# A two-layer decoder trunk on one core: the query transposes, two attention units, the value products and one bank choice are re-placed

## The chip, the core and the metric

The kernel runs on one core of a Trainium2 chip. The core has a matrix engine (TensorE, "PE" in the profile, with its weight loads shown apart as "PEld"), VectorE ("DVE"), ScalarE ("ACT"), GpSimd ("POOL") and SyncE ("SP"), which here only starts transfers. Each engine takes its instructions in the order of its own queue and waits where an operand or a buffer isn't ready. Matrix results go to an accumulator memory of eight banks; one bank holds 512 numbers of four bytes in each of 128 partitions. The metric is the device time of one execution in microseconds, lower is better.

## What is computed

Two layers over 256 tokens of width 2048, all in float32. In each layer one projection feeds a gated branch (A) and a windowed attention with 16 query heads on 4 key heads (B). Then follow an output projection and a SwiGLU block of width 5632.

```python
for l in range(DEPTH):
    h = rms_norm(x, norm1_g[l])
    z = h @ w_in[l]
    z_sgu = jax.nn.gelu(z[..., :2 * SGU_WIDTH], approximate=False)
    out_a = chunked_sgu(z_sgu, sgu_norm_g[l], sgu_w[l], sgu_b[l])
    out_b = swa_sink_attention(z[..., 2 * SGU_WIDTH:q_end], z[..., q_end:k_end],
                               z[..., k_end:], q_norm_g[l], k_norm_g[l], sinks[l],
                               rel_bias)
    mixed = jnp.concatenate([rms_norm(out_a, out_norm_a[l]),
                             rms_norm(out_b, out_norm_b[l])], axis=-1)
    x = x + mixed @ w_out[l]
    h2 = rms_norm(x, norm2_g[l])
    x = x + (jax.nn.silu(h2 @ w_gate[l]) * (h2 @ w_up[l])) @ w_down[l]
```

`chunked_sgu` normalizes its second half per head, multiplies it with a lower triangular 128x128 matrix per head (the gate product) and gates the first half with it. `swa_sink_attention` works in blocks of 128 queries: block 0 sees one block of keys, block 1 sees two; scores get a relative-position bias, the softmax has a sink term, and the value product follows.

## The kernel before, in words

**Products.** Every float32 weight tile of 256x512 is loaded (`raw`), rounded on ScalarE to a high part (`wh`, line 102), and VectorE takes the rest (`wl`, line 103). A product is three matmuls (lines 141 to 143). A unit (line 145) is one weight tile against two activations tiles and both token blocks: twelve matmuls of 512 columns. Each unit ends with `tick()`.

**Steps.** `later(delay, fn)` puts work into a list, and `tick` (line 124) runs what has come due, in order of time, then of entry. So the work between the large products is placed by unit counts. "Step k" below is the k-th unit after the first query block is done: 8 units for the second query block (steps 1 to 8), 8 each for the two blocks of the gate half (9 to 24), 8 each for the two blocks of the gated half (25 to 40), then the output projection. What is traced in this order is then put into queues by the language's scheduler, which may issue an instruction earlier where its operands and its buffer are free, and which assigns the slots of a tile's tag.

**The branch B.** `q_norm` (line 326) scales a query block, takes the inverse norms (a power on GpSimd, line 192), and transposes it in two pieces, five and six steps later (line 345); line 339 copies them out as `qT`. `attend(g, t)` (line 359) does group g of four heads on query block t: eight score matmuls into two half banks (lines 372 to 382), VectorE reads them with the bias (line 384), takes the maximum (389), ScalarE takes four exponentials (397), VectorE scales (406). `UNITS` (line 50) gives the step of each (g, t). After `LAG` = 5 steps `turn(b)` (line 408) transposes the probabilities of key block b into a bank, and ScalarE copies them out as `pts` (line 412). For each pair of groups `weigh(b)` (line 414) multiplies values and probabilities of both into `ov`, a bank of the `acc` tag, and `leave` (line 435) reads `ov` out with ScalarE and VectorE.

**The branch A.** `v_gate` (line 462) loads the triangular matrices (`wm`, lines 465 and 466), norms the block, and runs `spatial` (line 477) in two halves six and seven steps later: eight matmuls into `ps_g`, which VectorE reads in line 487. `u_gated` (line 502) transposes its result two and three steps later.

**The banks.** Five banks have the tag `acc`, two `dacc`, one `sm`. A projection block takes two `acc` banks, one for each token block. Everything small takes its bank from `small_ps` (line 136), which counts through `sm`, `dacc`, `acc`, `dacc`:

```python
pool, tag = ((pm, "sm"), (pd, "dacc"), (pa, "acc"), (pd, "dacc"))[next(turns) % 4]
```

So in one layer, steps 22 to 24 take in order: `s(2,1)` halves in `acc` and `dacc`, the first gate product in `sm`, the transposes of (2,0) in `dacc`, the second gate product in `acc` (step 23), the transposes of (3,0) in `dacc` (step 24), and then the next block's two `acc` banks. One layer counts 44 turns, so both layers meet the same banks.

**Buffers of attention.** The tag `spt` has four slots. Each unit takes one for its scores `s` (line 365); a unit with t = 1 takes a second one, `pt`, for its transposed probabilities (line 371).

**GpSimd's queue.** In order it holds the loads of the bias tiles (line 354; groups 2 and 3 come due with units (0,1) and (1,1)), of `wm`, and the powers of line 192.

Of the kernel before, what the change touches and what calls it, by code (L numbers as in the profile page):

```python
# [12 lines left out]
F32 = mybir.dt.float32  # L13
# [8 lines left out]
P = 128  # L22
D = 2048
SEQ = 256
NTOK = SEQ // P
L = 2
HD = 64
NH = 16
NKV = 4
GRP = NH // NKV  # L30
# [16 lines left out]
ACTS = 6  # L47
HOLD = 2
LAG = 5
UNITS = {(0, 0): 6, (1, 0): 8, (0, 1): 10, (1, 1): 13, (2, 0): 17, (3, 0): 19, (2, 1): 22, (3, 1): 26}  # L50
T3_DMA = ()
VEC = 1.14
VEC_P = 0.6
# [17 lines left out]
def trunk(ctx, tc, x, xt, w_in, w_out, w_gate, w_up, w_down, sgu_w, sgu_g, consts,  # L71
          rel_bias, onehot, radd, out):
    nc = tc.nc
# [8 lines left out]
    pa = ctx.enter_context(tc.tile_pool(name="pa", bufs=5, space=PSUM))  # L82
    pd = ctx.enter_context(tc.tile_pool(name="pd", bufs=2, space=PSUM))
    pm = ctx.enter_context(tc.tile_pool(name="pm", bufs=1, space=PSUM))
# [36 lines left out]
    def later(delay, fn):  # L121
        pending.append((clock[0] + delay, next(serial), fn))
# [10 lines left out]

    turns = itertools.count()

    def small_ps(shape, name):
        pool, tag = ((pm, "sm"), (pd, "dacc"), (pa, "acc"), (pd, "dacc"))[next(turns) % 4]
        return pool.tile(shape, F32, tag=tag, name=name)

    def mm3(acc, ah, al, wh, wl, first, last, **more):  # L140
# [142 lines left out]
    for lay in range(L):  # L283
# [11 lines left out]
        vhl = ap.tile([P, NTOK, NKV * HD], F32, tag="big", name="vhl", bufs=8)  # L295
# [30 lines left out]
        def q_norm(b, acc, lay=lay, layer=layer, qT=qT):  # L326
            qn = []
            for t in range(NTOK):
                z = zp.tile([P, NB], F32, tag="z", name="zq")
                nc.scalar.activation(z, acc[t], AF.Copy, scale=layer["rstd1"][t])  # L330
                qn.append(z)
            inv = head_inv(qn, 8)
            for t in range(NTOK):
                z3 = qn[t].rearrange("p (h d) -> p h d", d=HD)
                nc.vector.tensor_tensor(z3, z3, bc(inv[t], HD), ALU.mult)

            def to_T(c):
                ps = transpose_pair([qn[t][:, 2 * c * P : (2 * c + 2) * P] for t in range(NTOK)])
                nc.vector.tensor_scalar(
                    qT[b][:, 2 * c : 2 * c + 2, :], ps, cst[:, lay, C_QG : C_QG + 1], None,  # L340
                    ALU.mult,
                )

            for c in range(2):
                later(5 + c, lambda c=c: to_T(c))

        ov = {}
        sqs = zp.tile([P, 2 * NTOK, P], F32, tag="z", name="sqs")
# [8 lines left out]
        pts = {}  # L357

        def attend(g, t, kT=kT, qT=qT, vhl=vhl, ov=ov, bias=bias, layer=layer, pts=pts):
            nkb = t + 1  # L360
            nk = nkb * P
            k0 = SEQ - nk
            G = g // 2
            nsink = layer["nsink"]
            st = ap.tile([P, 2, GRP * P], F32, tag="spt", name="s", bufs=4)
            if t == 0:
                s = st[:, 0].rearrange("p (h k) -> p h k", k=nk)
                pts[g, t] = st[:, 1:2]
            else:
                s = st.rearrange("p b (h k) -> p (b h) k", k=nk)  # L370
                pts[g, t] = ap.tile([P, 2, GRP * P], F32, tag="spt", name="pt", bufs=4)
            halves = [small_ps([P, 2, nk], "ps_s") for r in range(2)]
            for i in range(2):
                for r in range(2):
                    h = g * GRP + 2 * i + r
                    nc.tensor.matmul(  # L376
                        halves[r][:, i, :],
                        qT[h // 8][HD * r : HD * r + HD, (h % 8) // 2, t * P : (t + 1) * P],
                        kT[HD * r : HD * r + HD, g, :nk],
                        start=True,  # L380
                        stop=True,
                    )
            for r in range(2):
                nc.vector.scalar_tensor_tensor(
                    s[:, r::2, :], halves[r], 1.0 / math.sqrt(HD), bias[g][:, r::2, k0:],
                    ALU.mult, ALU.add,
                )
            m = small([P, GRP], "m")
            nc.vector.tensor_reduce(m, s, AX.X, ALU.max)
            hs = slice(g * GRP, (g + 1) * GRP)  # L390
            nm = small([P, GRP], "nm")
            nc.vector.scalar_tensor_tensor(nm, m, -1.0, nsink[:, hs], ALU.mult, ALU.min)
            es = small([P, GRP], "es")
            nc.vector.tensor_tensor(es, nm, nsink[:, hs], ALU.subtract)
            den = small([P, GRP], "den")
            for i in range(GRP):
                nc.scalar.activation(
                    s[:, i, :], s[:, i, :], AF.Exp, bias=nm[:, i : i + 1],
                    accum_out=den[:, i : i + 1],
                )  # L400
            nc.scalar.activation(es, es, AF.Exp)

            rden = small([P, GRP], "rden")
            nc.vector.tensor_tensor(rden, den, es, ALU.add)
            nc.vector.reciprocal(rden, rden)
            nc.vector.tensor_tensor(s, s, bc(rden, nk), ALU.mult)

            def turn(b):
                pst = small_ps([P, GRP, P], "ps_p")
                for i in range(GRP):  # L410
                    nc.tensor.transpose(pst[:, i, :], s[:, i, b * P : (b + 1) * P], ident)  # L411
                nc.scalar.copy(pts[g, t][:, b], pst.rearrange("p h q -> p (h q)"))

            def weigh(b):
                if b == 0:
                    ov[G, t] = pa.tile([P, GRP * P], F32, tag="acc", name="ov")
                for k in range(2):
                    gk = 2 * G + k
                    nc.tensor.matmul(  # L419
                        ov[G, t][HD * k : HD * k + HD, :],  # L420
                        vhl[:, b, gk * HD : (gk + 1) * HD],
                        pts[gk, t][:, b],
                        start=b == 0,
                        stop=b == nkb - 1,
                        skip_group_check=True,
                    )
                if b == nkb - 1:
                    leave(G, t)

            for b in range(nkb):  # L430
                later(LAG + (2 if g % 2 else 1) * b, lambda b=b: turn(b))
                if g % 2:
                    later(LAG + 2 + 2 * b, lambda b=b: weigh(b))

        def leave(G, t, lay=lay, ov=ov, sqs=sqs, pairs_b=pairs_b):
            o = ov[G, t].rearrange("p (h q) -> p h q", q=P)
# [25 lines left out]
        def v_gate(b, acc, lay=lay, layer=layer, gate=gate):  # L462
            wm = ap.tile([P, 8, P], F32, tag="big", name="wm", bufs=8)
            with tc.issue_after(layer["anchor"].ins):
                nc.gpsimd.dma_start(wm, sgu_w[lay, :, 8 * b : 8 * b + 8, :])
            nc.gpsimd.affine_select(
                out=wm, in_=wm, pattern=[[0, 8], [1, P]], compare_op=ALU.is_ge, fill=0.0,
                base=0, channel_multiplier=-1,
            )
            gb = zp.tile([P, NB], F32, tag="z", name="gb")  # L470
            nc.gpsimd.dma_start(gb, sgu_g[lay, b * NB : (b + 1) * NB].partition_broadcast(P))

            v = ap.tile([P, NTOK, NB], F32, tag="big", name="v", bufs=8)
            vh = v.rearrange("p c (h d) -> p h c d", d=HD)
            gate[b] = v

            def spatial(half):
                hs = slice(4 * half, 4 * half + 4)
                ps = small_ps([P, 4, NTOK, HD], "ps_g")
                for h in range(4):  # L480
                    nc.tensor.matmul(
                        ps[:, h], wm[:, 4 * half + h, :], vh[:, 4 * half + h],
                        start=True, stop=True,
                    )
                sb = cst[:, lay, C_SB + 8 * b + 4 * half : C_SB + 8 * b + 4 * half + 4]
                for t in range(NTOK):
                    nc.vector.tensor_tensor(vh[:, hs, t], ps[:, :, t], bc(sb, HD), ALU.add)  # L487

            for t in range(NTOK):
                nc.scalar.activation(v[:, t], acc[t], AF.Gelu, scale=layer["rstd1"][t])  # L490
            inv = head_inv([v[:, t] for t in range(NTOK)], 8)
            for t in range(NTOK):
                v3 = v[:, t].rearrange("p (h d) -> p h d", d=HD)
                nc.vector.tensor_tensor(v3, v3, bc(inv[t], HD), ALU.mult)
                nc.vector.tensor_tensor(v[:, t], v[:, t], gb, ALU.mult)
            for half in range(2):
                later(6 + half, lambda half=half: spatial(half))
# [68 lines left out]
        acc = in_block(4)  # L566
# [339 lines left out]
```

## Time and profile before

| | us |
|---|---|
| time, median of 3 runs | 1936.86 |
| lowest and highest run | 1935.34 and 1938.22 |
| the profiled execution's own time | 1937.11 |
| its span in the profile | 1935.4 |

The span runs from the first to the last instruction; 1.7 us of the profiled execution lie around it. The profile gives busy time by engine, lists of who waited for whom, and a timeline of instructions; a row of the timeline has its start, its length, engine, line, operation, tiles and count, and in brackets the idle time just before it and what ended it. Rows of matmuls overlap, since they are pipelined, so the distance of two starts tells more than their length. The projection of layer 0 fills the span up to about 190 us, that of layer 1 about 985 to 1155 us, and the SwiGLU blocks take most of the rest.

### The profile page before, as it was taken

The page shows a single profiled execution, that of the slowest core. Times are in us where ns is not written, and L with a number is a line of the kernel's source. Part 1 is how long each engine was busy: PE and PEld are TensorE (multiplying, and loading weights), DVE is VectorE, ACT ScalarE, POOL GpSimd, SP SyncE. Part 2 cuts the span into 40 slices and gives each one's busy share as a digit, 9 for nine tenths or more (in the row PEclk, how much of TensorE's full clock was granted, in tenths as well). Part 3 has the DMA queues.
Part 4 walks back from the last instruction along what each step waited for, and adds up shares of the span by engine and source line. Part 5 has one row for each costly group of instructions (what it writes and reads, how often), then busy time and mean ns, then how long its engine had stood idle before and what let it go on. Part 6 is the DMA issues. An engine that isn't in the chain of part 4 may idle for free.

```text
span 1935.4 us, 24269 instructions
## 1 busy us (share of the span) xinstructions
PE 1923.8 (99%) x8734; PEld 1567.3 (81%) x8734; DVE 1699.1 (88%) x1896; ACT 1160.2 (60%) x1475; POOL 124.6 (6%) x127
## 2 busy tenths in 40 slices
PE   9999999999999999999999999999999999999999
PEld 7777888888888888888887788888888888888887
DVE  6787689999999999999767876899999999999995
ACT  7466566666565665656555665666665565665662
POOL 1210000000000000000012100000000000000000
PEclk9999999999999999999999999999999999999999
DMA  8744558668768777777655455576677678768773
GB/s 324 279 160 169 182 168 253 217 222 261 219 218 259 227 226 243 228 226 249 205 201 194 142 176 182 183 237 225 218 239 238 214 243 245 234 218 246 237 244 118
DMA packets 119704, 424.39 MB, mean 219 GB/s; under 512 B 13168, under 2 KB 15344, under 8 KB 119584
## 3 DMA queue, kind: packets, MB, share of 16 engines
q1 hardware_dynamic: 106928, 377.57, 54.0%
q0 software_dynamic: 12512, 45.19, 12.4%
q8 instruction: 68, 1.11, 0.2%
q14 instruction: 52, 0.43, 0.1%
q10 hardware_dynamic: 144, 0.08, 0.0%
HBM read 420.66 MB, written 4.23 MB: 220 GB/s over the span
## 4 chain that ended last, share of the span: by engine, by line
PE 96%; DVE 2%; ACT 1%; DMA 0%; issue 0%; SPq 0%; ACTq 0%; DVEq 0%
PE m L142 11%; PE m L143 11%; PE m L141 11%; PE acc L141 10%; PE dacc L141 10%; PE dacc L142 10%; PE acc L143 10%; PE acc L142 10%; PE dacc L143 10%; PE ps_f L214 1%; DVE wl L103 1%; PE ps_s L376 1%; PE ov L419 1%; PE ps_p L411 1%; PE ps_n L214 1%; ACT wh L102 0%
## 5 line engine op out<-in xcount | busy, mean ns | idle before, releaser
L102 ACT CAST wh<-raw 128x1024 fp32r<-128x1024 f32 (+1 forms) x778 | 799.0, 1049 | 583.5 <-DVE raw L674 198.8
L103 DVE TENSOR_TENSOR wl<-raw,wh 128x1024 fp32r<-128x1024 f32 (+1 forms) x778 | 926.4, 1219 | 131.1 <-ACT wh L102 125.3
L142 PE MATMUL dacc<-wl,aT 128*128 128x512 f32 x576 | 225.5, 391 | 0.0
L141 PE MATMUL dacc<-wh,aT 128*128 128x512 f32 x576 | 225.2, 392 | 0.0
L142 PE MATMUL m<-wl,ext 128*128 128x512 f32 x576 | 225.0, 391 | 0.0
L143 PE MATMUL dacc<-wh,aT 128*128 128x512 f32 x576 | 224.7, 390 | 0.0
L141 PE MATMUL m<-wh,ext 128*128 128x512 f32 x576 | 224.7, 392 | 0.0
L143 PE MATMUL m<-wh,ext 128*128 128x512 f32 x576 | 224.5, 390 | 0.0
L103 DVE TENSOR_TENSOR wl<-t,wh 128x1024 fp32r<-128x1024 f32 x144 | 175.6, 1222 | 25.0 <-ACT wh L102 21.3
L102 ACT CAST wh<-t 128x1024 fp32r<-128x1024 f32 x144 | 151.2, 1051 | 57.8 <-PE dacc L143 39.6
L141 PE MATMUL acc<-wh,hT 128*128 128x512 f32 x448 | 179.7, 402 | 2.2 <-DVE v L487 2.0
L142 PE MATMUL acc<-wl,hT 128*128 128x512 f32 x448 | 175.3, 391 | 1.2 <-DVE wl L103 1.2
L143 PE MATMUL acc<-wh,hT 128*128 128x512 f32 x448 | 175.3, 391 | 0.0
L141 PE MATMUL m<-wh,hT 128*128 128x512 f32 x432 | 168.6, 390 | 0.1
L143 PE MATMUL m<-wh,hT 128*128 128x512 f32 x432 | 168.2, 389 | 0.0
L142 PE MATMUL m<-wl,hT 128*128 128x512 f32 x432 | 168.2, 389 | 0.0
L141 PE MATMUL acc<-wh,aT 128*128 128x512 f32 x384 | 152.1, 396 | 0.0
L143 PE MATMUL acc<-wh,aT 128*128 128x512 f32 x384 | 150.1, 391 | 0.0
L142 PE MATMUL acc<-wl,aT 128*128 128x512 f32 x384 | 149.8, 390 | 0.0
L686 POOL DMA_DIRECT2D t<-in_w_gate_dram x72 | 61.5, 854 | 1325.9 <-DVE wl L103 828.0
L141 PEld LDWEIGHTS dacc<-wh,aT 128*128 128x128 f32 x576 | 108.2, 188 | 24.1 <-DVE xres L766 1.4
L142 PEld LDWEIGHTS dacc<-wl,aT 128*128 128x128 f32 x576 | 108.2, 188 | 24.0 <-DVE wl L103 2.2
(150 smaller groups left out, 2811.0 us busy)
## 6 DMA issues: line engine op xcount, KB each, us to landing
raw<-in_w_gate_dram SPq DMA_DIRECT2D x176, 512.0 KB, 5.4
raw<-in_w_up_dram SPq DMA_DIRECT2D x176, 512.0 KB, 4.5
raw<-in_w_down_dram SPq DMA_DIRECT2D x176, 512.0 KB, 4.9
raw<-in_w_in_dram SPq DMA_DIRECT2D x108, 512.0 KB, 4.2
t<-in_w_gate_dram POOLq DMA_DIRECT2D x72, 512.0 KB, 6.5
raw<-in_w_out_dram SPq DMA_DIRECT2D x64, 512.0 KB, 3.2
bias<-rdram POOLq DMA_DIRECT2D x8, 512.0 KB, 6.5
raw<-in_w_in_dram SPq DMA_DIRECT2D x8, 256.0 KB, 5.1
```

The source lines that it names most:

```text
L102: nc.scalar.copy(wh[:, j : j + step, :], src)
L103: nc.vector.tensor_tensor(wl[:, j : j + step, :], src, f(wh[:, j : j + step, :]), ALU.subtract)
L141: nc.tensor.matmul(acc, ah, wh, start=first, stop=False, **more)
L142: nc.tensor.matmul(acc, ah, wl, start=False, stop=False, **more)
L143: nc.tensor.matmul(acc, al, wh, start=False, stop=last, **more)
L214: nc.tensor.transpose(ps[:, j, t * P : (t + 1) * P], blocks[t][:, j * P : (j + 1) * P], ident)
L376: nc.tensor.matmul(halves[r][:, i, :], qT[h // 8][HD * r : HD * r + HD, (h % 8) // 2, t * P : (t + 1) * P], kT[HD * r : HD * r + HD, g, :n ...
L411: nc.tensor.transpose(pst[:, i, :], s[:, i, b * P : (b + 1) * P], ident)
L419: nc.tensor.matmul(ov[G, t][HD * k : HD * k + HD, :], vhl[:, b, gk * HD : (gk + 1) * HD], pts[gk, t][:, b], start=b == 0, stop=b == nkb - ...
L686: nc.gpsimd.dma_start(t2, w_gate[lay, b, i, 1], accum_op=ALU.add)
```

## The change

Four edits. The query transposes come four and five steps after `q_norm` instead of five and six. Unit (0,0) moves from step 6 to 5, unit (1,1) from 13 to 14; the load of group 3's bias comes due with the latter. The transposes of the second key block follow one step after the first for all groups (it was two for odd ones), and the value products of both key blocks run together, in one step, one step after the last transposes. The gate product passes `False` to `small_ps`, which then passes over a turn that falls on `acc`.

```diff
-UNITS = {(0, 0): 6, (1, 0): 8, (0, 1): 10, (1, 1): 13, (2, 0): 17, (3, 0): 19, (2, 1): 22, (3, 1): 26}
+UNITS = {(0, 0): 5, (1, 0): 8, (0, 1): 10, (1, 1): 14, (2, 0): 17, (3, 0): 19, (2, 1): 22, (3, 1): 26}
...
-    def small_ps(shape, name):
-        pool, tag = ((pm, "sm"), (pd, "dacc"), (pa, "acc"), (pd, "dacc"))[next(turns) % 4]
+    def small_ps(shape, name, spare=True):
+        at = next(turns) % 4
+        if at == 2 and not spare:
+            at = next(turns) % 4
+        pool, tag = ((pm, "sm"), (pd, "dacc"), (pa, "acc"), (pd, "dacc"))[at]
         return pool.tile(shape, F32, tag=tag, name=name)
...
             for c in range(2):
-                later(5 + c, lambda c=c: to_T(c))
+                later(4 + c, lambda c=c: to_T(c))
...
-            def weigh(b):
-                if b == 0:
-                    ov[G, t] = pa.tile([P, GRP * P], F32, tag="acc", name="ov")
-                for k in range(2):
-                    gk = 2 * G + k
-                    nc.tensor.matmul(
-                        ov[G, t][HD * k : HD * k + HD, :],
-                        vhl[:, b, gk * HD : (gk + 1) * HD],
-                        pts[gk, t][:, b],
-                        start=b == 0,
-                        stop=b == nkb - 1,
-                        skip_group_check=True,
-                    )
-                if b == nkb - 1:
-                    leave(G, t)
+            def weigh():
+                ov[G, t] = pa.tile([P, GRP * P], F32, tag="acc", name="ov")
+                for b in range(nkb):
+                    for k in range(2):
+                        gk = 2 * G + k
+                        nc.tensor.matmul(
+                            ov[G, t][HD * k : HD * k + HD, :],
+                            vhl[:, b, gk * HD : (gk + 1) * HD],
+                            pts[gk, t][:, b],
+                            start=b == 0,
+                            stop=b == nkb - 1,
+                            skip_group_check=True,
+                        )
+                leave(G, t)
 
             for b in range(nkb):
-                later(LAG + (2 if g % 2 else 1) * b, lambda b=b: turn(b))
-                if g % 2:
-                    later(LAG + 2 + 2 * b, lambda b=b: weigh(b))
+                later(LAG + b, lambda b=b: turn(b))
+            if g % 2:
+                later(LAG + 1 + nkb, weigh)
...
-                ps = small_ps([P, 4, NTOK, HD], "ps_g")
+                ps = small_ps([P, 4, NTOK, HD], "ps_g", False)
```

## The prediction, made before the changed kernel was built

> **What bounds the kernel now.** I read the page first: busy time by engine and the chain that ended last.
>
> ```profile
> PE 1923.8 (99%) x8734; PEld 1567.3 (81%) x8734; DVE 1699.1 (88%) x1896; ACT 1160.2 (60%) x1475; POOL 124.6 (6%) x127
> ...
> PE 96%; DVE 2%; ACT 1%; DMA 0%; issue 0%; SPq 0%; ACTq 0%; DVEq 0%
> ```
>
> TensorE works or streams for 1923.8 of 1935.4 us. The change removes no matmul, so it can only move the 11.6 us in which TensorE stood. Busy TensorE could hide slow spots, so I looked at the distance of starts in a plain stretch, and then at who TensorE waited for and at stretches around those waits.
>
> ```profile
> 1098.16 0.39 PE L141 MATMUL acc<-wh,hT 128*128 128x512 f32 x1
> 1098.39 0.39 PE L142 MATMUL acc<-wl,hT 128*128 128x512 f32 x1
> ...
> PE acc L141 <- DVE v L487: 2.0, 1, 2.0
> PE ps_t L214 <- DVE s L384: 1.7, 1, 1.7
> PE heat L172 <- DVE mhalf L174: 1.5, 1, 1.5
> PE acc L142 <- DVE wl L103: 1.2, 2, 0.6
> ...
> PEld ps_t L214 <- ACT s L412: 0.5, 1, 0.5
> ...
> 98.00:100.60 2.60, 0.86 (x5) 0.40 (x4) 2.53 (x5) 2.01 (x3) 0.88 (x2) 1.00 0.92 314
> 100.60:140.00 39.40, 39.40 (x204) 29.73 (x205) 34.23 (x64) 24.71 (x63) 5.62 (x4) 1.00 0.47 159
> 1100.50:1103.00 2.50, 0.47 (x3) 0.16 (x2) 2.22 (x9) 2.02 (x8) 0.00 (x0) 1.00 0.13 51
> 1900.00:1935.40 35.40, 30.89 (x137) 25.25 (x135) 15.56 (x18) 7.37 (x7) 0.00 (x0) 0.98 0.23 80
> ```
>
> A product takes 0.23 us from start to start; a unit of twelve is 2.7 us. (Columns of the last four rows: length, then busy us of PE, PEld, DVE, ACT, POOL, then granted clock.) Of the 11.6 us, 4.5 are the end of the kernel and 1.5 its beginning, out of reach. Within reach are two waits: 1.7 us, a query transpose that waits for VectorE to read scores (layer 0, step 14), and 2.0 us, the second bank of a new projection block, which waits for the gate product's read (layer 1, step 24). In both stretches VectorE is nearly full (2.53 of 2.60, 2.22 of 2.50): the bank is free late because VectorE takes its queue in order and comes late. So the ceiling is 1.74 + 2.03 = 3.8 us, or some 4.1 with the short wait for line 412 at step 14 of layer 1 (0.5 on the weight loads, about 0.3 of it in the products).
>
> **Layer 0: transposes earlier, (1,1) later.**
>
> ```profile
> 87.83 0.60 PE L411 MATMUL ps_p<-ident,s 128*128 128x128 f32 x4
> 95.40 0.60 PE L214 MATMUL ps_t<-ident,zq 128*128 128x128 f32 x4
> 100.48 0.66 PE L214 MATMUL ps_t<-ident,zq 128*128 128x128 f32 x4 [1.74 <-DVE s L384]
> ...
> 90.48 1.29 DVE L335 TENSOR_TENSOR zq<-zq,ir 128x512 f32<-128x512 f32 x2 [2.19 <-POOL ir L192]
> ...
> 99.75 1.28 DVE L384 SCALAR_TENSOR_TENSOR s<-ps_s,bias 128x512 f32<-128x512 f32 x2
> 100.94 0.74 DVE L339 TENSOR_SCALAR qT<-ps_t,cst 128x512 f32<-128x512 f32 x1
> ```
>
> The second transpose wants one of two `dacc` banks; one still holds the scores of (1,1), read from 99.75 on. With the transposes at steps 12 and 13 and (1,1) at 14 they no longer meet: -1.74. What is late next is the transposes' operand. Step 11 starts at 87.83, its four transposes take 0.36, so step 12 ends near 87.83 + 0.36 + 2.72 = 90.9, and VectorE finishes the scaled queries at 90.48 + 1.29 = 91.8, having waited 2.19 for GpSimd's power. That is a new wait of 0.9 at most; it is 0 if (0,0), a step earlier, takes its exponentials out of ScalarE's way before the query block is read. I take 0.5. The scores of (1,1) at step 14 (near 97.0) now want a `dacc` bank that step 12's transposes left; line 339 came 5.5 us after its transposes (95.40 to 100.94), so from 91.8 it would end at 98.1: 0 to 0.5 after the half that wants it, and I take 0, since it then stands ahead of (1,1)'s work. Layer 0: **-1.2**, from -1.7 to -0.3.
>
> **Layer 1: the bank counts shift.** Passing over `acc` uses up a turn, twice in layer 0 (second gate product of each block), so layer 1 starts two turns off and its small tiles sit in other banks than those of layer 0. Counted through the steps: the scores of (2,0) at step 17 start in `acc`; (3,0) at 19, and (2,1) at 22, start in the single `sm`; the first gate product is in `dacc`, the transposes of (2,0), same step, in `sm`, the second gate product in `dacc`; the transposes of (3,0) at 24 are in `acc`.
>
> ```profile
> 1078.78 0.71 PE L376 MATMUL ps_s<-kT,qT 64*128 64x128 f32 x8
> 1083.39 0.66 PE L411 MATMUL ps_p<-ident,s 128*128 128x128 f32 x4
> 1092.70 0.60 PE L411 MATMUL ps_p<-ident,s 128*128 128x128 f32 x4
> 1099.53 0.60 PE L411 MATMUL ps_p<-ident,s 128*128 128x128 f32 x4
> 1102.87 0.47 PE L141 MATMUL acc<-wh,hT 128*128 128x512 f32 x1 [2.03 <-DVE v L487]
> ...
> 1090.53 0.75 DVE L384 SCALAR_TENSOR_TENSOR s<-ps_s,bias 128x256 f32<-128x256 f32 x2
> 1097.30 1.28 DVE L384 SCALAR_TENSOR_TENSOR s<-ps_s,bias 128x512 f32<-128x512 f32 x2
> 1105.10 0.35 DVE L450 SCALAR_TENSOR_TENSOR aT<-ov,cst,aT 128x128 fp32r<-128x128 f32 x1
> 1106.75 0.58 ACT L412 COPY s<-ps_p 128x512 f32<-128x512 f32 x1
> ```
>
> Step 24: the wait for the gate product goes, -2.03. But the five `acc` banks then hold the old block (2), `ov` of (0,1) and the transposes of (3,0); the new block finds one bank, and its second one must come from `ov` (read until 1105.10 + 0.35) or from those transposes (copied until 1107.3), where it is due near 1100.6. If VectorE and ScalarE are as late as now, that is up to 4.8 in place of 2.03; the lower end is 0. For the choice I look at what makes VectorE late: TensorE gave the scores of (3,0) at 1078.78, and VectorE read them at 1090.53. Their `spt` slot explains it: in use are the scores of (1,1) (until their transposes at 1083.39), `pt` of (0,1) and of (1,1), and the scores of (2,0). After the change `pt` of (1,1) is first written at step 19, not 18, so (3,0) can take the fourth slot at once and its chain may start up to 4 us (1083.4 - 1079.4) sooner. So the read of `ov` should come sooner too; I take 1.0 for steps 22 to 24, nearer the low end.
>
> ```profile
> 1071.98 0.71 PE L376 MATMUL ps_s<-kT,qT 64*128 64x128 f32 x8
> ...
> 1072.55 0.69 ACT L490 ACTIVATE v<-acc,ir 128x512 f32<-128x512 f32 x1
> ```
>
> Step 17: two old banks, `ov` of (0,0) and two new ones fill `acc`, and the scores of (2,0) wait until ScalarE has read an old one: 1072.55 + 0.69 - 1071.98 = 1.3 at most, 0 if ScalarE comes sooner because (1,1)'s exponentials have moved; I take 0.6. Layer 1: -2.03 + 1.0 + 0.6 = **-0.4**, from -2.3 to +4.1.
>
> **What costs nothing.** The joined value products are the same matmuls; one place less per layer where small work breaks the stream is worth at most one product's distance, so 0 to -0.5 in all, taken as 0. The moved load and GpSimd's queue:
>
> ```profile
> 1023.99 1.54 POOL L354 DMA_DIRECT2D bias<-rdram  x2
> ...
> 1062.60 0.53 POOL L465 DMA_DIRECT2D wm<-in_sgu_w_dram  x1 [2.51 <-DVE s L384]
> 1066.57 1.54 POOL L466 TENSOR_SCALAR_AFFINE_SELECT wm<-wm 128x1024 f32<-128x1024 f32 x1 [3.43 <-DMA wm<-in_sgu_w_dram]
> ...
> 1076.84 2.92 POOL L192 TENSOR_TENSOR ir<-ms,mhalf 128x16 f32<-128x16 f32 x1 [8.73 <-DVE ms L190]
> ```
>
> Groups 2 and 3's bias leave at 1023.99, some 30 us before (1,1): they go when a slot is free, not at their step. The second `wm` load does wait for (1,1)'s read; a step (about 3.1 us) later its mask ends at 1071.2 instead of 1068.1, still ahead of the power at 1076.84, behind which nothing moves. Without that cover the power and VectorE behind it would be late by the rest.
>
> **Sum.** -1.2 - 0.4 = -1.6 on the profiled execution's 1937.11: **1935.5 us**. The median of the runs is 0.25 lower, well inside their spread, so I leave it there.
>
> **Rivals.** *All of it goes.* If no new wait opens, -4.1: 1933.0. For it: every new wait above has a lower end of 0, and layer 0's banks at step 24 are free. Against: VectorE's lateness isn't removed, only put before other banks.
>
> *The bank is filled again.* The gate product leaves the fifth bank and the transposes of (3,0) take it at step 24 of layer 1; the wait there stays at about 2, step 17 adds its 1.3, layer 0 gives -1.2: 1937.2. For it: the count of turns. Against: the earlier start of (3,0).
>
> *Slower: one bank twice in one step.* In layer 1, step 22 puts the scores of (2,1) and the transposes of (2,0) into the single `sm` bank. TensorE reached those transposes at 1092.70; VectorE read the first half of the scores until 1097.30 + 0.6 = 1097.9. A queue that is placed as now stands 5.2 us there, after which step 24 finds its bank free. With step 17's 1.3 and layer 0's -1.2: 1937.1 + 5.2 + 1.3 - 2.0 - 1.2 = 1940.4, and 1941.6 if layer 0 gives nothing. It is slower than before from a wait of 3.2 less step 17's part. For it: both rows; against: the scheduler may place the next unit's products ahead of those transposes. [...]
>
> **Numbers.** The forecast (some gain, partly given back) has 0.38 with a range of its own of 1933.5 to 1938; all of it goes 0.22; the bank is filled again 0.15; slower 0.25. 0.2% is 3.9 us, about what a measurement of this kernel can tell from no change. Below 1933.0 lie most of the second case's better half and a little of the forecast: 0.18. Above 1940.7 lie half of the slower case, 0.13, and 0.04 for what this reading doesn't foresee: 0.17. The rest, 0.65, is within. The range for 8 in 10 is 1932.4 to 1941.2.
>
> **What would show it.** Right: no wait of a query transpose for line 384 in layer 0, step 14; a short wait near step 12 with GpSimd's power behind it; no wait of `acc` for line 487; in layer 1 small waits at steps 17 and 22 to 24 on lines 490, 450 or 412; line 384 of (3,0) sooner after its scores. Wrong: a TensorE wait above 3 us at step 22 of layer 1 (slower case), no wait in either layer (the second case), or a change of time outside the two projections, which nothing here foresees.

## The result and the profile after

| | us |
|---|---|
| after, median of 12 runs | 1932.34 (1931.2 to 1933.7) |
| before, median of 12 runs on the same chip | 1936.35 (1934.72 to 1939.8) |
| ratio, 95% interval | 0.9979, 0.9972 to 0.9986 |
| the profiled execution after, its span | 1932.53, 1930.8 |

The change gains 4.0 us, 0.21%. The forecast was 1935.5, with 1932.4 as its low end: the sign was right, the size was not, and the time lies 0.06 us below the range. It is the first rival ("all of it goes", 1933.0) that came.

The page of the changed kernel: span, and busy time by engine.

```profile
span 1930.8 us, 24275 instructions
PE 1922.1 (100%) x8734; PEld 1568.0 (81%) x8734; DVE 1698.7 (88%) x1896; ACT 1162.8 (60%) x1475; POOL 122.8 (6%) x127
```

What TensorE waited for in it (total, times, longest):

```profile
PE heat L175 <- DVE mhalf L177: 1.5, 1, 1.5
PE acc L145 <- DVE wl L103: 1.1, 2, 0.6
PE acc L144 <- ACT pt L415: 0.4, 1, 0.4
PE dacc L144 <- ACT wh L102: 0.4, 1, 0.4
PE ps_p L414 <- DVE s L387: 0.4, 1, 0.4
```

Both long waits are gone. Three short ones, 0.4 each, came new: for `pt` and for `s` in the two projections, and for `wh` outside them, at 309.7 us. (Lines after the edit of `small_ps` count three higher: 387 reads scores, 415 copies `pt`.) The two stretches that the prediction showed, in its columns:

```profile
98.00:100.60 2.60, 2.60 (x15) 1.87 (x15) 2.60 (x3) 1.04 (x1) 0.00 (x0) 1.00 0.61 195
1100.50:1103.00 2.50, 2.50 (x12) 2.07 (x12) 2.46 (x4) 2.19 (x3) 0.00 (x0) 1.00 0.55 205
```

TensorE no longer stops in either, while VectorE is as full as it was (2.60 of 2.60, 2.46 of 2.50). It has not become faster; it comes sooner to what TensorE needs. Layer 1's timeline, steps 19 to 22, shows where:

```profile
1076.54 0.72 PE L379 MATMUL ps_s<-kT,qT 64*128 64x128 f32 x8
1086.46 1.14 PE L379 MATMUL ps_s<-kT,qT 64*128 64x256 f32 x8
1087.53 1.94 PE L422 MATMUL ov<-pt,vhl 128*64 128x512 f32 x8
1089.40 1.16 PE L483 MATMUL ps_g<-v,wm 128*128 128x128 f32 x8
1090.91 0.66 PE L414 MATMUL ps_p<-ident,s 128*128 128x128 f32 x4 [0.36 <-DVE s L387]
...
1080.13 0.42 DVE L387 SCALAR_TENSOR_TENSOR s<-ps_s,bias 128x256 f32<-128x256 f32 x1
1090.17 1.28 DVE L387 SCALAR_TENSOR_TENSOR s<-ps_s,bias 128x512 f32<-128x512 f32 x2
```

The scores of (3,0) are read 3.59 us after TensorE starts them (1076.54 to 1080.13; before 1078.78 to 1090.53, 11.75), those of (2,1) 3.71 us after (before 1089.50 to 1097.30, 7.80). Below, "the lag" of a unit is this distance, in layer 1. From the first transposes of k to the sum of squares at the end of the branch, layer 0 takes 132.70 us (before 134.54) and layer 1 145.18 (before 148.26). That is -1.8 and -3.1; the rest of the program changes by less than 0.4. Against a second profile of the kernel before (before_again, below) it is +0.1 and -4.7: how the gain divides between the layers depends on the execution.

### The profile page after: what moved, and what is told of

Same layout as the page of the kernel before. It is cut to its first block, busy times and chain, and to the rows that moved or that the text cites. A ratio compares the mean times of both kernels' runs of the same rounds, so it can differ in the third digit from the quotient of the medians.

```text
span 1930.8 us, 24275 instructions
## 1 busy us (share of the span) xinstructions
PE 1922.1 (100%) x8734; PEld 1568.0 (81%) x8734; DVE 1698.7 (88%) x1896; ACT 1162.8 (60%) x1475; POOL 122.8 (6%) x127
## 4 chain that ended last, share of the span: by engine, by line
PE 94%; DVE 3%; ACT 1%; issue 1%; DMA 1%; POOL 0%; SPq 0%; ACTq 0%; DVEq 0%; POOLq 0%
PE m L145 11%; PE m L146 11%; PE m L144 11%; PE dacc L144 10%; PE dacc L145 10%; PE dacc L146 10%; PE acc L144 9%; PE acc L146 9%; PE acc L145 9%; DVE wl L103 1%; PE ps_f L217 1%; PE ps_n L217 1%; PE ps_s L379 0%; PE ps_p L414 0%; PE ov L422 0%
```

## The experiments

Each run was compared with the kernel before on the same chip; its medians there were 1936.38, 1937.16 and 1937.63 in the three groups, so ratios compare better than times. The layers' columns are the lengths just defined, from the profiled execution.

| run | median us (runs) | ratio, 95% interval | layer 0 | layer 1 | lag (3,0) | lag (2,1) |
|---|---|---|---|---|---|---|
| moves_only | 1945.84 (5) | 1.0049, 1.0035 to 1.0063 | 140.64 | 150.83 | 3.59 | 6.46 |
| join_only | 1933.73 (11) | 0.9985, 0.9976 to 0.9994 | 132.10 | 146.70 | 7.54 | 6.79 |
| bank_only | 1941.07 (11) | 1.0024, 1.0015 to 1.0033 | 132.59 | 153.97 | 10.44 | 6.54 |
| all_but_bank | 1931.41 (8) | 0.9974, 0.9964 to 0.9984 | 132.60 | 144.62 | 3.59 | 3.71 |
| split_early | 1940.63 (11) | 1.0017, 1.0008 to 1.0025 | 138.04 | 148.02 | 3.74 | 2.37 |
| join_late | 1938.59 (11) | 1.0010, 1.0001 to 1.0019 | 137.15 | 148.82 | 3.75 | 7.72 |
| split_late | 1940.13 (11) | 1.0014, 1.0005 to 1.0023 | 137.51 | 149.19 | 3.77 | 7.45 |
| join_first | 1932.99 (8) | 0.9976, 0.9966 to 0.9986 | 133.46 | 145.64 | 7.05 | 6.76 |
| join_second | 1934.00 (8) | 0.9976, 0.9966 to 0.9986 | 133.59 | 145.95 | 4.19 | 4.31 |
| join_bank | 1941.34 (12) | 1.0018, 1.0010 to 1.0026 | 134.58 | 153.91 | 6.25 | 6.76 |
| before_again | 1936.64 (1) | none | 132.57 | 149.84 | 11.75 | 7.80 |
| after_again | 1932.22 (1) | none | 132.76 | 145.19 | 3.60 | 3.71 |

Theory A: VectorE came late because (3,0) had to wait for a slot of `spt`, and the moves end that. Theory B: the wait in layer 1 is only the gate product's place in `acc`, and the bank edit ends it.

**moves_only**: the query transposes and the two units, nothing else.

```diff
-UNITS = {(0, 0): 6, (1, 0): 8, (0, 1): 10, (1, 1): 13, (2, 0): 17, (3, 0): 19, (2, 1): 22, (3, 1): 26}
+UNITS = {(0, 0): 5, (1, 0): 8, (0, 1): 10, (1, 1): 14, (2, 0): 17, (3, 0): 19, (2, 1): 22, (3, 1): 26}
...
-                later(5 + c, lambda c=c: to_T(c))
+                later(4 + c, lambda c=c: to_T(c))
```

> Only the query transposes and the units (0,0) and (1,1) are moved; value products split and gate product in acc as before. Both theories: the wait of 1.7 us in layer 0 (query transposes for the read of scores) goes, about -1.8 us in layer 0. Theory A (VectorE's lateness, caused by the missing fourth spt slot, makes the wait of layer 1): (3,0) finds its slot at step 19 and is read under 5 us after its scores, but the last value products come at step 23 and hold slots and ov longer, so the wait at step 24 of layer 1 is between 0 and 3 us. Theory B (the wait of layer 1 is only the gate product's place in acc): it stays at 2.0 us. Time 1933 to 1936 by A, 1934.5 by B.

It is 9.5 us slower than before: both theories miss the time. No wait at step 24 came, which B had at 2.0 and A between 0 and 3. The timeline around step 21 of layer 0 (TensorE, and ScalarE's copy):

```profile
123.23 1.07 PE L419 MATMUL ov<-pt,vhl 128*64 128x512 f32 x2
124.24 0.66 PE L411 MATMUL ps_p<-ident,s 128*128 128x128 f32 x4
...
127.53 1.07 PE L419 MATMUL ov<-pt,vhl 128*64 128x512 f32 x2 [1.71 <-ACT pt L412]
...
126.90 1.06 ACT L412 COPY pt<-ps_p 128x512 f32<-128x512 f32 x2
```

Now (3,0) takes the free slot (lag 3.59, as A said), and `pt` of (1,1) must wait for the slot that (1,1)'s own scores hold until their second transposes at 124.24. With the split order, these come at step 21 together with the value product of the first key block, half of which stands and waits. The two copies then leave ScalarE in one go, at 126.90, behind the exponentials of (3,0) in its queue. The scores of (2,1), a step behind, find the slots held until step 23: VectorE stands idle for 3.34 us and reads them only when the last value product is done.

```profile
135.91 1.08 PE L419 MATMUL ov<-pt,vhl 128*64 128x512 f32 x4
...
137.03 1.29 DVE L384 SCALAR_TENSOR_TENSOR s<-ps_s,bias 128x512 f32<-128x512 f32 x2 [3.34 <-PE ov L419]
```

From that comes a second wait, 2.16 in each layer, of the second block's gate product (step 30). And here two matmuls of a value product take 1.01 us (123.23 to 124.24), since the pairs of the two groups are torn apart. In the kernel before, four, both groups together, take as long (1090.69 to 1091.70):

```profile
1090.69 1.08 PE L419 MATMUL ov<-pt,vhl 128*64 128x512 f32 x4
1091.70 1.16 PE L481 MATMUL ps_g<-v,wm 128*128 128x128 f32 x8
```

**join_only**: transposes at `LAG + b`, value products in one step (the change's hunk of `weigh`).

> Only the value products are joined; (1,1) then has its second transposes at step 19 instead of 20. Both theories: the 1.7 us wait of layer 0 stays. Theory A: the slot for the scores of (3,0) comes free a step sooner, they are read some 3 us sooner than before, and the wait at step 24 of layer 1 falls from 2.0 to under 0.7 us. Theory B: it stays at 2.0 us, since the gate product is still in acc. Time near 1934 by A with fewer places where small work breaks the stream, near 1936 by B.

0.9985. No wait at step 24 is left, as A had it. The second transposes of (1,1) come one step sooner, so does the last value product (step 21, not 22), and the slots with them: the lag of (3,0) falls from 11.75 to 7.54. The wait of layer 0 is gone too, which neither theory had; see before_again.

**bank_only**: the change's hunk of `small_ps` and its call.

> Only the gate product passes over acc. Both theories: the 1.7 us wait of layer 0 stays. Theory A: VectorE is as late as before, so in layer 1 a wait of 1.5 us or more comes at steps 22 to 24 in another bank (the transposes of (2,0) in sm, or the new block's acc). Theory B: the 2.0 us go and nothing comes in their place. Time 1936 to 1939 by A, 1934.4 by B.

The wait came as theory A said; the time lies 2 us above its range. What TensorE waited for:

```profile
PE ps_p L414 <- DVE s L387: 4.0, 1, 4.0
PE heat L175 <- DVE mhalf L177: 1.5, 1, 1.5
PE ps_s L379 <- ACT v L493: 1.4, 1, 1.4
```

This is the prediction's slower rival, with its two waits at steps 22 (priced 5.2, came 4.04) and 17 (priced 1.3, came 1.44). Windows behind the long one, in the prediction's columns, the granted clock third from the end:

```profile
1093.00:1097.00 4.00, 0.78 (x5) 0.78 (x5) 4.00 (x6) 1.78 (x4) 0.00 (x0) 0.74 0.39 126
1097.00:1101.00 4.00, 4.00 (x12) 3.13 (x11) 3.21 (x8) 2.46 (x9) 0.00 (x0) 0.50 0.44 137
```

Twelve matmuls in 4.00 us instead of 2.7, at a granted clock of 0.50: the wait costs some 2 us more than its length, an estimate from half of these 4.00 us.

**all_but_bank**: the changed kernel with the gate product back in `acc` (`small_ps([P, 4, NTOK, HD], "ps_g")`).

> The changed kernel with the gate product in acc again. Theory A: VectorE is in time, the gate product's read comes right after its matmuls, and step 24 of layer 1 waits under 0.5 us; time as the changed kernel, 1932 to 1933. Theory B: the wait of about 2 us at step 24 of layer 1 is back; time near 1934.4.

0.9974 (1931.41, 0.6 below A's range), no wait at step 24: B falls. Against join_only in the same group the moves are worth 2.3 us here; against moves_only the joined products are worth 14.4. Its interval overlaps that of the whole change, so the bank edit is worth nothing that was measured; without it the wait of 0.36 at step 22 is absent.

What was left: is it the time at which slots come free (theory C), or the fewer stops of joined products (theory D)? Three kernels, all with the moves and the earlier transposes and without the bank edit, shift or split the value products of the units with t = 1: joined at step 22 is all_but_bank.

**split_early**: `weigh(b)` as in the kernel before, its blocks at steps 21 and 22.

```diff
-            if g % 2:
-                later(LAG + 1 + nkb, weigh)
+                if g % 2:
+                    later(LAG + 2 + b, lambda b=b: weigh(b))
```

> The moves with the transposes of (1,1) at steps 19 and 20 as in the changed kernel, but its value products split again: the first block at step 21, the second at 22; gate product in acc as before. Theory C (release): what counts is when the four spt slots come free, and whether a value product stands ahead of the transpose that frees its own slot. Here the slots come free at step 22 as in the kernel without the bank edit (1931.41), so (3,0) is read within 4.5 us of its delivery, (2,1) within 5, and no gate product waits for VectorE; but ScalarE copies pt of (1,1) at 125.9, behind the exponentials of (3,0), and the first value product, due near 123.3, has to wait some 1 to 2.7 us for it in each layer: 1933.5 to 1937.5. Theory D (fewer stops): the joined products are worth their stops, and without them the time is that of the moves alone, 1944 to 1947.

The lags came as C said, and so did the wait of the first value product (2.02 and 1.60), with none at the gate product. But the time is 3 us above C's range. One part is the torn pair, 1.0 in each layer, the other the clock behind the 2.02, granted at 0.52:

```profile
129.00:132.00 3.00, 3.00 (x9) 2.37 (x8) 1.46 (x2) 0.00 (x0) 0.00 (x0) 0.52 0.90 311
```

Nine matmuls in 3.00 us where thirteen fit, 0.23 apart. Against D: by the lengths of the two layers it is 5.4 us faster than the moves alone, though it is split like them. Layer 1 is 3.4 longer than in all_but_bank; the 1.60 and the torn pair make 2.6 of that, and where the rest comes from is open.

**join_late**: joined, both blocks at step 23.

```diff
-                later(LAG + 1 + nkb, weigh)
+                later(LAG + 2 * nkb, weigh)
```

> The same moves, value products joined, but those of (1,1) and (3,1) one step later (at 23 and 35) so that pt and the scores of the next unit come free a step later. Theory C: (2,1) is read about 6.5 us after its delivery, not 4.4 to 4.9; the gate product of the second block (step 30) waits 1.5 to 2.5 us in each layer for VectorE, and the clock falls to about 0.8 for some 5 us behind it, so some 3 to 5 us for each layer: 1937 to 1942, though every product is joined. No wait of a value product for ScalarE's copy. Theory D: the time of the joined moves, 1930.5 to 1933.

The clearest of the runs: the same joined products one step later cost 7 us against all_but_bank (1.0010 against 0.9974). The lag of (2,1) is 7.72, and the step-30 gate product waits in both layers:

```profile
PE ps_g L483 <- DVE nm L395: 4.2, 2, 2.1
```

The clock behind the first of them, 0.57 over 4.00 us (about 0.8 was expected):

```profile
154.00:156.00 2.00, 1.42 (x11) 1.26 (x11) 2.00 (x6) 1.55 (x7) 0.00 (x0) 1.00 0.00 0
156.00:160.00 4.00, 4.00 (x11) 3.14 (x12) 4.00 (x8) 1.34 (x6) 0.00 (x0) 0.57 0.74 206
160.00:162.00 2.00, 2.00 (x11) 1.62 (x10) 1.97 (x4) 1.32 (x2) 0.00 (x0) 1.00 0.80 315
```

C was right within its range, D is out. No run gave the tag a fifth slot, which would test C from the other side.

**split_late**: split, blocks at steps 22 and 23.

```diff
-                    later(LAG + 2 + b, lambda b=b: weigh(b))
+                    later(LAG + 2 + t + b, lambda b=b: weigh(b))
```

> The same moves, value products of the units with t = 1 split, first block at step 22, second at 23: late enough that no copy is awaited, and the slots free at step 23. Theory C: as the joined products at step 23, plus 0 to 1.5 us for the four added stops; no wait of a value product for ScalarE's copy, a wait of 1.5 to 2.5 us at the gate product of the second block in each layer: 1937 to 1943. Theory D: the time of the moves alone, 1944 to 1947.

The same waits (2.14 and 2.17), and as in moves_only VectorE stands idle until the last value product releases its read of (2,1), 2.49 and 2.81 us. The length is 0.4 us more in each layer than join_late. That is what joining is worth by itself; their intervals overlap, so the two layers' lengths bear it, not the times.

**before_again**: the kernel before, unchanged.

> The kernel before, unchanged, profiled a second time. If the wait of 1.74 us for the scores' read in layer 0 (step 14) is a matter of the run, it is absent or shorter than 1 us here, and the power on GpSimd before it takes 2.9 us, not 3.95; if it belongs to the program it is there again with 1.5 to 2.0 us. The wait of 2.03 us in layer 1 at step 24 is there in either case, 1.8 to 2.3 us.

1936.64 us, span 1934.9. The wait of layer 0 is not there; the one of step 24 is there with the same 2.03, but now the clock behind it is 0.54 over 3.00 us. The power before step 10 and the window behind the wait; first this execution, then the one that the prediction read:

```profile
85.02 2.92 POOL L192 TENSOR_TENSOR ir<-ms,mhalf 128x16 f32<-128x16 f32 x1 [23.93 <-DVE ms L190]
...
1102.00:1105.00 3.00, 3.00 (x9) 2.32 (x8) 2.68 (x5) 2.97 (x5) 0.00 (x0) 0.54 0.00 0
```

```profile
86.50 3.95 POOL L192 TENSOR_TENSOR ir<-ms,mhalf 128x16 f32<-128x16 f32 x1 [25.41 <-DVE ms L190]
...
1102.00:1105.00 3.00, 2.13 (x9) 1.80 (x10) 2.25 (x7) 2.98 (x11) 0.00 (x0) 1.00 0.00 0
```

In the second execution nine matmuls came at half speed, about 1.6 us lost, and nothing of that in the first. So of one program one execution lost 1.74 + 2.03, the other 2.03 + 1.6.

The traces show where layer 0 parts. A cast of ScalarE and VectorE's subtraction at the power, in this execution and then in the first:

```profile
71.34 1.05 ACT L102 CAST wh<-raw 128x1024 fp32r<-128x1024 f32 x1 [1.66 <-PE acc L143]
...
85.09 1.23 DVE L103 TENSOR_TENSOR wl<-raw,wh 128x1024 fp32r<-128x1024 f32 x1
```

```profile
73.05 1.05 ACT L102 CAST wh<-raw 128x1024 fp32r<-128x1024 f32 x1 [1.18 <-DMA raw<-in_w_in_dram]
...
86.46 1.21 DVE L103 TENSOR_TENSOR wl<-raw,wh 128x1024 fp32r<-128x1024 f32 x1
```

In the first, weight tiles landed later and ScalarE waited for them until 73.05, so the power started 1.5 us later (86.50, not 85.02). There the subtraction of line 103 had begun 0.04 us before the power, which took 3.95; here it began 0.07 us after, and the power took 2.92 (last section). The runs of the kernel before spread over 4 to 7 us in each group, those of the changed one over 2.5.

**join_first** and **join_second**: the joined products with one half of the moves each, to tell C from theory E, that the query transposes are what the moves bring.

join_first moves the transposes and (0,0):

```diff
+UNITS = {(0, 0): 5, (1, 0): 8, (0, 1): 10, (1, 1): 13, (2, 0): 17, (3, 0): 19, (2, 1): 22, (3, 1): 26}
...
+                later(4 + c, lambda c=c: to_T(c))
```

> The joined value products with only the first half of the moves: query transposes one step earlier and (0,0) at 5; (1,1) stays at 13, gate product in acc. Theory C (release of the spt slots) says that the moves work through (1,1): its pt takes a slot only once the scores of (3,0) have theirs. Here that is not so: (3,0) of layer 1 is still read some 7 to 8 us after its delivery as with the joined products alone, and the time is theirs within 1 us, 1932.7 to 1934.7. Theory E (the query transposes are what the moves are worth): the time of the joined moves, 1930.5 to 1932.4.

join_second moves (1,1) alone:

```diff
+UNITS = {(0, 0): 6, (1, 0): 8, (0, 1): 10, (1, 1): 14, (2, 0): 17, (3, 0): 19, (2, 1): 22, (3, 1): 26}
```

> The joined value products with only the second half of the moves: (1,1) at 14; query transposes and (0,0) as before, gate product in acc. Theory C: (3,0) of layer 1 is read within 4.5 us of its delivery and (2,1) within 5, no wait at step 24, and the time is that of the joined moves, 1930.7 to 1932.7. Theory E: that of the joined products alone, 1933 to 1934.7.

The lags came as C said (7.05; 4.19 and 4.31), the times did not separate: 0.9976 both. The median of join_first lies in C's range, that of join_second (1934.00) in E's. In join_second (1,1) at 14 meets query transposes at 13 and 14, which the whole change avoids, and a product waits for `pt` in each layer, 1.39 and 1.01:

```profile
PE acc L141 <- ACT pt L412: 2.4, 2, 1.4
```

So with the joined products in place, the moves' halves are worth little each, and E can't be told from C by time.

**join_bank**: the joined products and the bank edit, no moves.

> The joined value products and the gate product off acc, without the moves. Theory C: the scores of (3,0) in layer 1 are read some 7 us late and those of (2,1) with them, so at step 22 the transposes of (2,0), which want the same single sm bank, stand for 2 to 4 us, and the clock may halve behind that for up to 2 us more: 1935.5 to 1940. Theory B (the gate product's place in acc is what costs): 1931.5 to 1934.

C had the waits right and B falls; the time, 1941.34, lies 1.3 us above C's range. With a lag of 6.25 instead of 3.59 the bank edit brings back both waits of the slower rival, 4.34 and 1.45. In layer 0 the wait of 1.76, which C didn't count, is there again, and the power before it took 3.95.

```profile
PE ps_p L414 <- DVE s L387: 4.3, 1, 4.3
PE ps_t L217 <- DVE s L387: 1.8, 1, 1.8
```

**after_again**: the changed kernel, unchanged.

> The changed kernel, profiled a second time. If the change has taken the long waits away, and not only this one time, no product or transpose of the two projections waits more than 0.7 us after the first block, the granted clock stays at 1.00 there, and the time lies within 1931.2 to 1934. If a wait of 1.5 us or more, or a stretch at half clock, shows in either projection, the changed kernel has the same uncertain waits as the one before, only more seldom.

1932.22 us; no wait above 0.64 in the projections, and the clock at 1.00.

## Why the prediction was right or wrong

**The bound** was read rightly: both waits hung on VectorE being late, and in layer 1 it was late through the slots of `spt`; in layer 0 it was late because weight tiles and the power were. What a wait is worth was not: 1.74 + 2.03 counts what one execution showed. Of the five profiles that place layer 0's units and query transposes as before, the first is there in the two in which the power took 3.95 us (before, join_bank) and absent in the three with 2.92; the second cost 2.03 in one execution and some 3.6 in another. The prediction set the ceiling at 4.1, and its windows had the clock at 1.00 at both waits; for the second of them that held in one execution of two. Waits of 2.02 to 2.17 were followed by half clock in seven cases of nine (last section), and so were those of 4.04 (bank_only, granted 0.50) and 4.34 (join_bank, matmuls 0.43 us apart).

**Layer 0, -1.2.** The new wait of step 12, taken as 0.5, did not come. The rows after the change:

```profile
87.11 0.69 DVE L338 TENSOR_TENSOR zq<-zq,ir 128x512 f32<-128x512 f32 x1 [2.82 <-POOL ir L195]
87.79 0.69 DVE L338 TENSOR_TENSOR zq<-zq,ir 128x512 f32<-128x512 f32 x1
...
91.19 0.60 PE L217 MATMUL ps_t<-ident,zq 128*128 128x128 f32 x4
```

The scaled queries are there at 88.5, 2.7 us ahead of need: the chain ran 3.4 us sooner (90.48 before). The prediction gave (0,0), a step earlier, as the reason for its lower end and then paid half of the wait; but 2.5 of the 3.4 lie between the two executions of the kernel before (90.48 and 87.97), so its 0.9 came from a late execution. A wait of 0.43 for `pt` came instead, which it didn't name. Measured -1.8 against the first execution and +0.1 against the second, which lost nothing here.

**Layer 1, -0.4.** The new waits of step 17 (0.6) and steps 22 to 24 (1.0) came as 0 and 0.36. The reason was in the text: (3,0) takes the slot at once and comes up to 4 us sooner. It came 8 us sooner (lag 11.75 to 3.59, and 3.59 with the moves alone): the 4 us were counted to the release at 1083.39, but VectorE's read stood in its queue for 7 us more (1090.53), and that goes too. So the step that VectorE's lateness "isn't removed, only put before other banks" failed: it is removed. In the sum this is the term that is off, 1.6 given back where 0.36 came. Measured -3.1, and -4.7 against the second execution.

**"What costs nothing", the joined products: the other step that failed.** They were priced as the same matmuls with one stop less, 0 to -0.5, taken as 0. As an edit alone they are the only one that gains (0.9985, -2.7 us), and not by the stop (0.4 in each layer): `turn` of the second key block and the last value product come one step earlier than in the split order, and free the slots that the next scores wait for. And without them the moves lose 9.5 us; on top of the moves they are worth 14.4 (1945.84 to 1931.41). The prediction saw that `pt` and scores compete for four slots, and did not ask, for the second edit, when it gives its slot back. The moved load and GpSimd's queue cost nothing, as said.

**The rivals.** "All of it goes" came near in its number (1933.0), in part by luck: it takes 1.74 from layer 0, which one execution of the kernel before lost and the other did not, and it takes 2.3 from layer 1, which gained 3.1 or more. "The bank is filled again" did not come, since VectorE was no longer late. The slower one was a true mechanism, met at its place and near its price in bank_only and join_bank; the moves and the joined products together keep it away in the changed kernel, where 0.36 of it is left. The bank edit, which the change of banks in the prediction dwelt on most, is not needed: all_but_bank (0.9974) does as well.

**The sum.** The parts alone give +9.5, -2.7 and +4.7; together they give -4.0. No sum over edits would have found that. Nor does a lag alone tell a run's time: join_only (7.54 and 6.79) is faster than moves_only (3.59 and 6.46). What tells it is which instruction on TensorE stands behind a late release, run by run.

What stays open: why the weight tiles land later in one execution than in the next, and how often; and how the last 1 us of layer 1's gain splits between fewer stops and the waits on weights.

## What to carry to other kernels

Where an engine comes late to a bank, look for the buffer whose release it waits for, and follow who holds each slot step by step, before and after each edit; a move of one step can be worth 7 us or nothing by which release it shifts. Price an edit together with the others that touch the same slots, not alone. Take a second profile of the kernel before a wait is counted: here one wait came and went, and the other cost between 2.0 and 3.6 us.

## What the hardware showed unexpectedly

**The clock.** Nine waits of TensorE between 2.0 and 2.2 us stand in the traces. Seven were followed by a stretch at half clock, with matmuls 0.43 us apart instead of 0.23: 2.02 (split_early), 2.03 (before_again), 2.06 and 2.09 (join_late), 2.14 and 2.17 (split_late), and 2.16 in layer 0 of moves_only. By the granted clock the stretch lasted about 3.4 us in before_again (0.56 and 0.59 in the two halves of 1102 to 1106) and in join_late behind the 2.06 (0.57 over 156 to 160). Two waits were not followed by one: 2.03 in the first profile of the kernel before, and 2.16 in layer 1 of moves_only. Nor was any wait of 1.76 or less in the projections. The two equal waits of moves_only, layer 0 and then layer 1:

```profile
158.00:161.00 3.00, 2.90 (x12) 2.83 (x13) 3.00 (x7) 2.90 (x11) 0.00 (x0) 0.51 0.19 38
...
1125.00:1127.00 2.00, 1.62 (x11) 1.46 (x12) 2.00 (x6) 1.75 (x7) 0.00 (x0) 1.00 0.00 0
```

So the length of a wait did not decide it alone: 2.03 was followed by half clock in one execution of the kernel before and not in the other, and 2.16 in one layer of moves_only and not in the other. What did decide it was not shown.

**The power on GpSimd.** On 128x16 numbers the power of line 192 (195 after the edit) takes 3.76 to 3.95 us in all 53 cases of the 14 profiles in which VectorE's subtraction of line 103 is running when it starts, and 2.90 to 2.94 in the other 59.
